# Attention of a two-layer trunk in one-engine steps, score banks used for transposes too, and a later start of branch B

## The chip, the cores and the metric

The kernel runs on one NeuronCore of a Trainium2 chip. The metric is the device time of one execution in microseconds (us), lower is better. One execution was also taken by the hardware profiler; every row below is from that one.

## What is computed

Two layers of a decoder trunk on 256 tokens of width 1024, all in float32: a SwiGLU half step, a mixer of three token branches, another SwiGLU half step, each followed by a layer norm. The mixer, cut to what matters here:

```
parts = split(x @ w_in)                      # one projection, columns shared out to A, B, C and gates
A: 3 groups of 12 heads, (window, stride) = (128,1), (512,4), (2048,16); the groups' outputs
   are combined by their softmax denominators
B: 16 query heads on 2 key heads, window 128, one learned sink per head
C: retention in chunks, then y_c = silu(parts_cg) * normed(r)
merged = g_a*(y_a @ w_proj_a) + g_b*(y_b @ w_proj_b) + g_c*(y_c @ w_proj_c);  out = merged @ w_out
```

A and B are softmax attention: scores q.k, a mask with a maximum per row, exp with a sum per row, scaling, then weights times values. A weight matrix of probabilities is transposed on TensorE (PE) before it meets the values.

## The kernel before

**The weight stream.** All the large products are cut into units: four 128-row blocks of a weight matrix, 512 columns wide (1 MB). For each unit the SP queue loads it (`dma_until`), ScalarE (ACT) rounds it to `wh` (`hi_until`, L279, "hi" below), VectorE (DVE) makes the rest `wl = ws - wh` (`lo_until`, L289, "lo" below), and PE runs three products per block. `mm_unit` (L293 to L325) is one half unit: a unit for one half of its output (t = 0 or 1), 24 matmuls of 256 columns or 12 of 512. hi and lo run three units ahead: hi stands at the end of a unit's first half, lo at the end of the second. In the mixer of one layer there are 72 units, in this order: C's values, queries and keys, B's queries, B's keys and values (`bkv`), C's swish gate (`cg`, two chunks of two units), then A's queries and keys (`aqk`, nine chunks; each ends in two rotary steps on DVE, L523 to L543, "rope" below) with A's values (`av0`, `avf`) between, then B's output projection, B's merge gates, C's gates and projection, A's gates and projection, and the last projection.

**The attention tasks.** Attention is written as Python generators. After the matmuls of a half unit, `tick` (L203) moves each running generator on to its next `yield`, and so writes its instructions on all engines right there. Each engine runs its instructions in the order in which they were written, and waits on the others by semaphores. `b_pair` (L777) is two heads of B, eight pairs per layer; `a_quad` (L695) four heads of A, three quads per layer. A pair starts at least four half units after the last start, a quad when no pair or quad runs. In a pair, the scores (PE), the masks (DVE, L639) and the exps (ACT, L643) are all written in one half unit; two half units on the scaling (ACT, L802), two further on four transposes and their copy, one on two more and their copy. A quad does the same in larger steps: near scores of two head pairs (L648), far scores (L665), the combining factors (L713 to L725), 16 scalings (L732, L736), transposes in three half units, then the values (L751).

**Banks.** Of the eight PSUM banks four (`acc`) hold the running products, one (`T`) takes transposes, two (`S`) take scores, one (`U`) takes weights times values. In `a_quad` the second transposes of a step already go to an `S` bank; in `b_pair` all go to `T`.

**The start of B.** `done_bkv` (L578) queues the eight pairs, so the first runs during the units of the swish gate `cg`. C's transposed output is queued at the first unit of gate (2, 0), L305.

Of the kernel before, what the change touches and what calls it, by code (L numbers as in the profile page):

```python
# [75 lines left out]
def mixer_chunks():  # L76
# [8 lines left out]
    aqk = lambda s, g: out.append(("aqk", (s, g), np.concatenate([roped(a_cols(3 * g, s)), roped(a_cols(3 * g + 1, s))])))  # L85
    out.append(("bkv", 0, np.concatenate([roped(OFF_KB + np.arange(128)), OFF_KB + 128 + np.arange(128), a_cols(2, 0)])))
    for n in range(2):
        out.append(("cg", n, OFF_CG + 512 * n + np.arange(512)))
    for s in range(3):
# [72 lines left out]
class Kernel:  # L162
# [4 lines left out]
    def __init__(self, ctx, tc, a):  # L167
# [12 lines left out]
        self.last = -3  # L180
# [22 lines left out]
    def tick(self, half):  # L203
# [89 lines left out]
    def mm_unit(self, u, t, mid=None, tick=False):  # L293
# [7 lines left out]
        if k0 == 0 and t == 0:  # L301
# [3 lines left out]
            elif ch["kind"] == "gate" and ch["arg"] == (2, 0):  # L305
# [272 lines left out]
    def done_bkv(self, ch, t, ps):  # L578
        nc = self.nc
        if t == 1:  # L580
            self.y[0] = self.new_y("p (b t) -> p b t", 8)
            nc.scalar.activation(self.y[0][:, 6:8], ps.rearrange("p (t c) -> p t c", t=2), AF.Copy)
            for n in range(2):
                for b in range(4):
                    self.queue(self.b_pair(n, b), "pair")
# [33 lines left out]

    def transpose_p(self, P, lo, hi, spare=False):  # L620
# [3 lines left out]
        for i in range(lo, hi):  # L624
            nc.tensor.transpose(ps[:, 128 * (i - lo):128 * (i - lo) + 128], P[:, 128 * i:128 * i + 128], self.ident)  # L625
        nc.scalar.activation(P[:, 128 * lo:128 * hi], ps[:, :128 * (hi - lo)], AF.Copy)
# [21 lines left out]
    def near_scores(self, s, b, stat):  # L648

        nc = self.nc  # L650
        k = self.aqk[s, 0]
        Sp = self.pair_scores(k[:, b], k[:, 2 + b])
# [5 lines left out]
        nc.vector.tensor_scalar(stat[:, 0, :, 2 * b:2 * b + 2], mx, -0.125, None, op0=OP.mult)  # L658
# [4 lines left out]
        return P  # L663

    def far_scores(self, s, stat):  # L665

        nc = self.nc
        Sp = self.two_S()
        for b in range(2):
            for rp in range(2):  # L670
                for g in range(2):
                    k = self.aqk[s, g + 1]
                    c0 = 256 * b + 128 * rp + 64 * g
                    for e in range(2):
                        for c in range(2):
                            r = slice(64 * e, 64 * e + 64)
                            tq = slice(64 * (2 * rp + c), 64 * (2 * rp + c) + 64)
                            nc.tensor.matmul(Sp[e][64 * c:64 * c + 64, c0:c0 + 64], k[r, b, tq], k[r, 2 + b, tq],
                                             start=True, stop=True)
        P = self.far_probs()  # L680
        mx = self.sml.tile([128, 2, 4], F32, name="fx")
        for b in range(2):
            for e in range(2):
                h = 2 * b + e
                for rp in range(2):
                    c0 = 256 * b + 128 * rp
                    self.masked(P[:, 256 * h + 128 * rp:256 * h + 128 * rp + 128], Sp[e][:, c0:c0 + 128],
                                self.mask[:, 256:384], mx[:, rp, h:h + 1])
        nc.vector.tensor_scalar(stat[:, 0], mx, -0.125, None, op0=OP.mult)
        for h in range(4):  # L690
            for rp in range(2):
                self.exp(P[:, 256 * h + 128 * rp:256 * h + 128 * rp + 128], stat[:, 0, rp, h:h + 1], stat[:, 1, rp, h:h + 1])
        return P

    def a_quad(self, s):  # L695
        nc = self.nc
# [4 lines left out]
                  for r in range(4) for t in range(2)]  # L701
        P = []
        for b in range(2):
            P.append(self.near_scores(s, b, near))
            yield
            yield
        for rows, t, to, rp in places:
            nc.gpsimd.tensor_copy(moved[to, :, rp], near[rows, :, t])
        F = self.far_scores(s, far)
        yield  # L710
        yield
        top = self.sml.tile([128, 2, 4], F32, name="top", bufs=2)
        nc.vector.tensor_tensor(top, moved[:, 0], far[:, 0], op=OP.min)  # L713
        for g, x in enumerate((moved, far)):
            nc.vector.tensor_tensor(f[:, g], top, x[:, 0], op=OP.subtract)
        nc.scalar.activation(f, f, AF.Exp)
        for g, x in enumerate((moved, far)):
# [15 lines left out]
        for h in range(4):  # L733
            for rp in range(2):
                sl = F[:, 256 * h + 128 * rp:256 * h + 128 * rp + 128]
                nc.scalar.activation(sl, sl, AF.Copy, scale=f[:, 1, rp, h:h + 1])  # L736
        yield
        yield
        for x, n in ((P[0], 6), (P[1], 6), (F, 8)):
            x = x.rearrange("p e k -> p (e k)") if n == 6 else x  # L740
            self.transpose_p(x, 0, 4)
            self.transpose_p(x, 4, n, spare=True)
            yield
        yield
        self.a_values(s, P, F)

    def a_values(self, s, P, F):
# [4 lines left out]
        for b in range(2):  # L752
# [12 lines left out]
        nc.scalar.activation(self.y[0][:, 2 * s:2 * s + 2].rearrange("p b (a r) -> p b r a", r=4),  # L765
                             U.rearrange("p b (r a) -> p b r a", r=4), AF.Copy)
# [10 lines left out]
    def b_pair(self, n, b):  # L777

        nc, l = self.nc, self.layer
        Sp = self.pair_scores(self.bq[n][:, b], self.kb[:, n])  # L780
        P = self.b_p[n, b] = self.probs((4 * n + b) % 3 == 2)
# [7 lines left out]
        nc.vector.tensor_scalar(nm, mx, -1.0, None, op0=OP.mult)  # L789
        for e in range(2):  # L790
# [5 lines left out]
        yield  # L796
# [305 lines left out]
```

## Time and profile before

| | us |
|---|---|
| median of 3 runs | 1771.24 |
| lowest and highest | 1770.83, 1771.26 |
| the profiled execution, its own time | 1771.4 |
| its span, first to last instruction | 1769.3 |
| PE busy | 1702.9 (96%) |
| DVE busy | 1064.7 (60%) |
| ACT busy | 840.0 (47%) |

The two mixers lie in the stretches 285 to 605 and 1165 to 1485 us of the span; the rest is the SwiGLU steps. A timeline row reads: start, length, engine, line, operation, tile written <- tiles read, shape, count, and in brackets how long the engine had been idle before it and what ended that. A row of a window table gives for each engine its busy time and instruction count, then PEclk (the share of TensorE's full clock of 2.4 GHz that was granted, 0.50 being 1.2 GHz).

### The profile page before, as it was taken

To read this page: it belongs to the slowest core of one execution; us is meant where nothing else is said; L and a number is where in the kernel's file an instruction comes from. 1 tells how busy PE (TensorE), PEld (TensorE's weight loads), DVE (VectorE), ACT (ScalarE), POOL (GpSimd) and SP (SyncE) were. 2 spreads that over 40 slices of the span, in tenths; PEclk is the share of its full clock that TensorE was granted. 3 is DMA by queue.
4 is the path that set the end of the run, shared out by engine and by line. 5 is a ranking of instruction groups with operands and counts; after the bars stand their busy time and mean duration, and the time that the engine had idled before them with its cause. 6 is when DMAs were issued, how large, how long until landed. Compare 5 with 4: busy or idle time off the path is not lost.

```text
span 1769.3 us, 29021 instructions
## 1 busy us (share of the span) xinstructions
PE 1702.9 (96%) x12325; PEld 1546.8 (87%) x12325; DVE 1064.7 (60%) x1536; ACT 840.0 (47%) x1207; POOL 93.1 (5%) x176
## 2 busy tenths in 40 slices
PE   9999999999889999999999999999998899999997
PEld 7998898878779998999899988978788789979985
DVE  5555677667564558554565546867666545675544
ACT  5444434654665544444344434355645675444431
POOL 0000001010211000000000000010101200000000
PEclk9999999899999999999999999999999999999998
DMA  7555543343434455555455465343433434555451
GB/s 287 214 187 193 209 162 123 139 155 121 163 118 149 171 184 193 196 210 201 167 190 211 173 222 193 143 143 121 154 141 137 165 112 180 203 184 214 175 209 47
DMA packets 49138, 303.38 MB, mean 171 GB/s; under 512 B 7025, under 2 KB 7281, under 8 KB 15089
## 3 DMA queue, kind: packets, MB, share of 16 engines
q1 hardware_dynamic: 44640, 294.12, 45.5%
q0 software_dynamic: 4224, 7.35, 1.2%
q8 instruction: 96, 1.57, 0.3%
q14 instruction: 34, 0.27, 0.0%
q10 hardware_dynamic: 144, 0.07, 0.0%
HBM read 297.31 MB, written 1.05 MB: 169 GB/s over the span
## 4 chain that ended last, share of the span: by engine, by line
PE 66%; DVE 17%; ACT 13%; issue 3%; DMA 0%; POOL 0%; SPq 0%; POOLq 0%; ACTq 0%
PE acc L320 63%; DVE wl L289 6%; ACT wh L279 5%; DVE an L639 1%; DVE slab L543 1%; ACT an L643 1%; DVE rt L523 1%; DVE rt L525 1%; DVE rt L524 1%; ACT an L802 1%; ACT af L643 1%; ACT an L732 1%; PE U L751 1%; ACT af L736 1%; DVE af L639 1%
## 5 line engine op out<-in xcount | busy, mean ns | idle before, releaser
L320 PE MATMUL acc<-xT,wh 128*128 128x256 f32 x4800 | 851.1, 280 | 0.0
L289 DVE TENSOR_TENSOR wl<-ws,wh 128x2048 fp32r<-128x2048 f32 (+1 forms) x277 | 615.5, 2240 | 269.5 <-ACT wh L279 267.7
L320 PEld LDWEIGHTS acc<-xT,wh 128*128 128x128 f32 x4800 | 736.9, 189 | 0.2
L320 PE MATMUL acc<-xT,wl 128*128 128x256 f32 x2400 | 680.1, 283 | 1.3 <-DVE wl L289 1.3
L279 ACT ACTIVATE wh<-ws 128x2048 fp32r<-128x2048 f32 (+1 forms) x277 | 518.4, 1873 | 247.1 <-PE acc L320 205.2
L320 PEld LDWEIGHTS acc<-xT,wl 128*128 128x128 f32 x2400 | 454.8, 189 | 8.9 <-issue 5.6
L320 PE MATMUL acc<-wh,xT 128*128 128x512 f32 (+1 forms) x832 | 266.5, 395 | 0.2
L320 PE MATMUL acc<-wh,hT 128*128 128x512 f32 x704 | 222.7, 396 | 0.0
L320 PEld LDWEIGHTS acc<-wh,xT 128*128 128x128 f32 x832 | 157.2, 191 | 39.9 <-issue 4.3
L320 PE MATMUL acc<-wl,xT 128*128 128x512 f32 (+1 forms) x416 | 163.1, 392 | 0.2 <-DVE wl L448 0.2
L320 PEld LDWEIGHTS acc<-wh,hT 128*128 128x128 f32 x704 | 132.4, 188 | 31.5
L320 PE MATMUL acc<-wl,hT 128*128 128x512 f32 x352 | 139.2, 395 | 0.0
L320 PE MATMUL acc<-slab,wh 128*128 128x256 f32 x704 | 127.6, 285 | 0.9 <-DVE slab L448 0.6
L490 DVE TENSOR_TENSOR h<-sa,acc 128x512 f32<-128x512 f32 x36 | 24.7, 686 | 154.2 <-PE acc L320 154.2
L320 PEld LDWEIGHTS acc<-slab,wh 128*128 128x128 f32 x704 | 110.3, 194 | 2.0 <-DVE slab L448 2.0
L320 PE MATMUL acc<-slab,wl 128*128 128x256 f32 x352 | 101.3, 288 | 7.2 <-ACT slab L447 7.2
L487 ACT ACTIVATE sa<-acc 128x512 f32<-128x512 f32 x36 | 21.5, 597 | 158.5 <-PE acc L320 158.5
L320 PEld LDWEIGHTS acc<-wl,xT 128*128 128x128 f32 x416 | 79.6, 191 | 16.7 <-DVE wl L448 0.5
L320 PEld LDWEIGHTS acc<-wl,hT 128*128 128x128 f32 x352 | 66.2, 188 | 15.6
L320 PEld LDWEIGHTS acc<-slab,wl 128*128 128x128 f32 x352 | 67.9, 193 | 9.9 <-ACT slab L447 8.6
L574 POOL DMA_DIRECT2D va<-slab x96 | 51.3, 538 | 240.7 <-ACT slab L570 238.4
L625 PE MATMUL T<-ident,an 128*128 128x128 f32 x120 | 25.6, 317 | 31.1 <-ACT an L732 12.2
(177 smaller groups left out, 1244.7 us busy)
## 6 DMA issues: line engine op xcount, KB each, us to landing
ws<-in_w_dram SPq DMA_DIRECT2D x265, 1024.0 KB, 4.8
ws<-in_w_dram SPq DMA_DIRECT2D x12, 512.0 KB, 4.2
ws<-in_w_dram SPq DMA_DIRECT2D x12, 256.0 KB, 5.7
va<-slab POOLq DMA_DIRECT2D x96, 32.0 KB, 3.0
gain<-in_ln_g_dram SPq DMA_DIRECT2D x4, 512.0 KB, 5.7
gain<-in_ln_b_dram SPq DMA_DIRECT2D x4, 512.0 KB, 7.2
slab<-in_decay_dram POOLq DMA_DIRECT2D x4, 512.0 KB, 4.6
x<-in_x_dram SPq DMA_DIRECT2D x4, 256.0 KB, 6.1
```

The lines of the kernel that those rows point to most:

```text
L279: self.nc.scalar.activation(wh[:, :n], self.staged[v][:, :n], AF.Copy)
L289: self.nc.vector.tensor_tensor(wl[:, :n], ws[:, :n], wh[:, :n].bitcast(F32), op=OP.subtract)
L320: nc.tensor.matmul(ps[:, c0:c1], a, b, start=first, stop=last, skip_group_check=len(parts) > 1)
L487: nc.scalar.activation(self.sa, ps, AF.Silu)
L490: nc.vector.tensor_tensor(h, self.sa, ps, op=OP.mult)
L523: nc.vector.stream_shuffle(t2, ps, SWAP)
L524: nc.vector.tensor_tensor(t1, ps, trig(self.cos), op=OP.mult)
L525: nc.vector.tensor_tensor(t2, t2, trig(self.sin), op=OP.mult)
L574: nc.gpsimd.dma_start(self.vf[s][p0:p0 + 32, r], self.stage[r::4, t, g])
L625: nc.tensor.transpose(ps[:, 128 * (i - lo):128 * (i - lo) + 128], P[:, 128 * i:128 * i + 128], self.ident)
L639: self.nc.vector.tensor_tensor_reduce(out=P, in0=Sp, in1=mask, op0=OP.add, op1=OP.max, scale=1.0, scalar=-3e38, accum_out=mx)
L643: self.nc.scalar.activation(P, P, AF.Exp, bias=nm, scale=0.125, accum_out=den)
```

## The change

Five things change, all in the mixer.

1. `b_pair` and `a_quad` are cut into steps of one engine each: scores in one half unit, masks in the next, exps in the next, and so on. A quad takes 15 half units from its scores to its values.
2. Starts are spaced by a table, `room`: after a pair the next pair may start three half units later and a quad seven; after a quad the next quad 15.
3. Transposes of `b_pair` go to both a lent `S` bank and `T` in the same half unit, and are copied out in the next half unit, the `S` bank first. `a_quad` packs its transposes in the same way.
4. The eight pairs are queued at the last swish gate (`done_cg`, n = 1, t = 1) instead of at `bkv`.
5. C's transposed output is queued at gate (1, 0) instead of gate (2, 0).

```
-        if kind and {"two": half == 1, "pair": self.now >= self.last + 4, "quad": not self.pairs}[kind]:
+        if kind and (half == 1 if kind == "two" else self.now >= self.room[kind]):
 ...
-            self.last = self.now
+            if kind != "two":
+                self.room = {"pair": self.now + 3, "quad": self.now + (7 if kind == "pair" else 15)}
...
-            elif ch["kind"] == "gate" and ch["arg"] == (2, 0):
+            elif ch["kind"] == "gate" and ch["arg"] == (1, 0):
                 self.queue_yT(2, 8)
...
+    def transposes(self, groups, spare):
+        ps = self.p1.tile([128, 512], F32, name="S", bufs=2) if spare else self.pt.tile([128, 512], F32, name="T")
+        copies, c = [], 0
+        for P, lo, hi in groups:
+            n = 128 * (hi - lo)
+            for i in range(lo, hi):
+                nc.tensor.transpose(ps[:, c + 128 * (i - lo):c + 128 * (i - lo) + 128], P[:, 128 * i:128 * i + 128], self.ident)
+            copies.append((P[:, 128 * lo:128 * hi], ps[:, c:c + n]))
+            c += n
+        return lambda: [nc.scalar.activation(d, x, AF.Copy) for d, x in copies]
...  a_quad:
         for b in range(2):
-            P.append(self.near_scores(s, b, near))
+            Sp = self.pair_scores(k[:, b], k[:, 2 + b])
             yield
+            P.append(self.near_max(Sp, b, near))
             yield
-        for rows, t, to, rp in places:
-            nc.gpsimd.tensor_copy(moved[to, :, rp], near[rows, :, t])
-        F = self.far_scores(s, far)
-        yield
+            self.near_exp(P[b], b, near)
+        move(0)
+        Sp = self.far_scores(s)
+        yield
+        F = self.far_max(Sp, far)
+        move(1)
         yield
...
+        for h, rp, sl in self.FAR:
+            self.exp(F[:, sl], far[:, 0, rp, h:h + 1], far[:, 1, rp, h:h + 1])
+        yield
         nc.scalar.activation(f, f, AF.Exp)
+        yield
...
+        yield
+        a = self.transposes([(x[0], 0, 4)], False), self.transposes([(x[0], 4, 6), (x[1], 0, 2)], True)
+        yield
+        for c in a:
+            c()
+        a = self.transposes([(x[1], 2, 6)], True)
+        yield
+        a()
+        a = self.transposes([(F, 0, 4)], False), self.transposes([(F, 4, 8)], True)
+        yield
+        for c in a:
+            c()
+        yield
+        U = self.a_values(s, P, F)
+        yield
...  b_pair:
         Sp = self.pair_scores(self.bq[n][:, b], self.kb[:, n])
+        yield
         P = self.b_p[n, b] = self.probs((4 * n + b) % 3 == 2)
...
         nc.vector.tensor_scalar(nm, mx, -1.0, None, op0=OP.mult)
+        yield
...
-        self.transpose_p(x, 0, 4)
-        yield
-        self.transpose_p(x, 4, 6)
+        a = self.transposes([(x, 4, 6)], True), self.transposes([(x, 0, 4)], False)
+        yield
+        for c in a:
+            c()
...  done_cg:
+        if n == 1 and t == 1:
+            for i in range(2):
+                for b in range(4):
+                    self.queue(self.b_pair(i, b), "pair")
```

What this moves, at three places. All rows are the order in which an engine's instructions stand; `an` and `af` are probabilities, `bnm` the negated row maximum of a pair, `near` and `far` the row statistics of a quad, `rt` a merge gate, `wh` the rounded weights. Line numbers shift between the two (hi L279 and L280, lo L289 and L290, exp L643 and L646, copies of transposes L626 and L629).

ACT during branch B, before: from one hi to the next, with the four-transpose copy of one pair and the exps of the next.

```order
L279 ACTIVATE wh<-ws 128x2048
L626 ACTIVATE an<-T 128x512
L643 ACTIVATE an,bden<-an,bnm 128x128
L643 ACTIVATE an,bden<-an,bnm 128x256
L794 ACTIVATE bes<-bmx,sink 128x2
```

The same place in the changed kernel, the exps of one pair and the copies of the pair ahead of it:

```order
L646 ACTIVATE an,bden<-an,bnm 128x128
L646 ACTIVATE an,bden<-an,bnm 128x256
L815 ACTIVATE bes<-bmx,sink 128x2
L629 ACTIVATE an<-S 128x256
L629 ACTIVATE an<-T 128x512
L280 ACTIVATE wh<-ws 128x2048
```

The exps now stand ahead of the copies, both copies stand together, and the one out of the `S` bank is new.

DVE in the middle of a quad, before: from the lo of one unit to the end of the combining factors (`moved` is `near` brought to the far rows' partitions by GpSimd, `aw` and `top` are factors).

```order
L289 TENSOR_TENSOR wl<-ws,wh 128x2048
L713 TENSOR_TENSOR top<-moved,far 128x8
L715 TENSOR_TENSOR af<-top,moved 128x8
L715 TENSOR_TENSOR af<-top,far 128x8
L718 TENSOR_TENSOR aw<-af,moved 128x8
L718 TENSOR_TENSOR aw<-af,far 128x8
L719 TENSOR_TENSOR top<-aw 128x8
L720 RECIPROCAL top<-top 128x8
L722 TENSOR_TENSOR af<-af,top 128x8 x2
```

The same in the changed kernel:

```order
L290 TENSOR_TENSOR wl<-ws,wh 128x2048
L722 TENSOR_TENSOR top<-moved,far 128x8
L724 TENSOR_TENSOR af<-top,moved 128x8
L724 TENSOR_TENSOR af<-top,far 128x8
L290 TENSOR_TENSOR wl<-ws,wh 128x2048
L731 TENSOR_TENSOR aw<-af,moved 128x8
L731 TENSOR_TENSOR aw<-af,far 128x8
L732 TENSOR_TENSOR top<-aw 128x8
L733 RECIPROCAL top<-top 128x8
L735 TENSOR_TENSOR af<-af,top 128x8 x2
```

A lo stands now between the two parts, so that ACT's exp of `af`, which lies between them, has a half unit of its own.

ACT in the third quad, where B's merge gates (sigmoid) run as well, before: from the exp of the factors to the second gate.

```order
L716 ACTIVATE af<-af 128x16
L725 ACTIVATE fn<-af 32x4 x8
L934 ACT_TABLE_LOAD
L934 ACTIVATE rt<-acc,gbias 128x256 x2
L279 ACTIVATE wh<-ws 128x2048
L934 ACTIVATE rt<-acc,gbias 128x256 x2
```

In the changed kernel, from the far exps of that quad to the fourth gate:

```order
L646 ACTIVATE af,far<-af,far 128x128 x8
L960 ACT_TABLE_LOAD
L960 ACTIVATE rt<-acc,gbias 128x256 x2
L280 ACTIVATE wh<-ws 128x2048
L728 ACT_TABLE_LOAD
L728 ACTIVATE af<-af 128x16
L960 ACT_TABLE_LOAD
L960 ACTIVATE rt<-acc,gbias 128x256 x2
```

Exps and sigmoids alternate here, with a table load at each turn: five loads per layer at the gates instead of one. At the swish gates four fewer stand, so that the program has 16 loads before and 16 after.

## Rows read from the trace of the kernel before

**Rows 1.** Window table of three stages: first mixer, SwiGLU steps between, second mixer.

```profile
285.00:605.00 320.00, 295.50 (x2327) 263.31 (x2326) 197.41 (x436) 191.16 (x411) 37.31 (x75) 0.96 0.39 138
605.00:1165.00 560.00, 559.71 (x3865) 515.28 (x3864) 337.09 (x334) 228.85 (x189) 12.01 (x12) 1.00 0.52 190
1165.00:1485.00 320.00, 294.35 (x2347) 262.45 (x2347) 194.61 (x425) 190.72 (x409) 34.34 (x74) 0.96 0.40 143
```

**Rows 2.** Waits of PE, first mixer: releaser, us in total, times, longest.

```profile
PE T L625 <- ACT an L732: 6.1, 2, 3.6
PE T L625 <- ACT an L802: 5.8, 4, 2.5
PE T L625 <- ACT an L626: 3.8, 3, 1.6
PE acc L320 <- ACT slab L447: 3.6, 2, 3.4
```

**Rows 3.** Timeline of PE: two waits in the first mixer, and what follows one.

```profile
326.07 1.30 PE L625 MATMUL T<-ident,an 128*128 128x128 f32 x4 [2.48 <-ACT an L802]
...
581.91 0.66 PE L625 MATMUL T<-ident,an 128*128 128x128 f32 x4 [1.55 <-ACT an L626]
...
582.55 0.36 PE L320 MATMUL acc<-xT,wl 128*128 128x256 f32 x1
```

**Rows 4.** PE in windows of 1 us: busy time (count), PEclk, DMA share, GB/s.

```profile
326.00:327.00 1.00, 0.93 (x4) 0.50 0.98 139
...
333.00:334.00 1.00, 1.00 (x11) 1.00 0.91 369
...
582.00:583.00 1.00, 1.00 (x10) 1.00 0.00 0
```

**Rows 5.** Timeline of DVE in the third quad: the lo of two units.

```profile
546.99 2.29 DVE L289 TENSOR_TENSOR wl<-ws,wh 128x2048 fp32r<-128x2048 f32 x1 [3.82 <-ACT wh L279]
...
554.87 2.29 DVE L289 TENSOR_TENSOR wl<-ws,wh 128x2048 fp32r<-128x2048 f32 x1 [4.28 <-ACT wh L279]
```

**Rows 6.** Timeline of ACT between them: near exps, a copy, the hi.

```profile
550.69 0.40 ACT L643 ACTIVATE an<-an,near 128x128 f32<-128x128 f32 x1 [3.73 <-DVE near L658]
...
552.46 0.58 ACT L945 ACTIVATE y<-acc 128x512 f32<-128x512 f32 x1
552.94 1.90 ACT L279 ACTIVATE wh<-ws 128x2048 fp32r<-128x2048 f32 x1
```

**Rows 7.** Timeline of DVE in branch B: masks, two ropes, lo, sums.

```profile
331.14 0.28 DVE L639 CUSTOM_DVE_ANT_0 af<-S,mask 128x128 f32<-128x128 f32 x1
...
332.97 0.74 DVE L523 STREAM_SHUFFLE rt<-acc 128x512 f32<-128x512 f32 x1
...
338.56 2.29 DVE L289 TENSOR_TENSOR wl<-ws,wh 128x2048 fp32r<-128x2048 f32 x1
340.76 0.16 DVE L797 TENSOR_TENSOR bden<-bden,bes 128x4 f32<-128x4 f32 x1
```

**Rows 8.** Timeline of ACT in branch B: a pair's exps, then the hi.

```profile
333.09 0.40 ACT L643 ACTIVATE af<-af,bnm 128x128 f32<-128x128 f32 x1 [2.41 <-DVE bnm L789]
...
335.24 1.90 ACT L279 ACTIVATE wh<-ws 128x2048 fp32r<-128x2048 f32 x1
```

**Rows 9.** Timeline of PE at full clock: values, scores, two half units, scores.

```profile
426.97 1.52 PE L819 MATMUL U<-an,vb 128*64 128x256 f32 x16
428.42 0.93 PE L634 MATMUL S<-slab 64*128 64x128 f32 x8
429.28 0.50 PE L320 MATMUL acc<-wh,xT 128*128 128x512 f32 x1
...
435.08 0.93 PE L634 MATMUL S<-slab 64*128 64x128 f32 x8
```

**Rows 10.** Timeline of ACT at the first merge gate: table load, sigmoids.

```profile
569.83 1.28 ACT L934 ACT_TABLE_LOAD   x1
571.12 0.84 ACT L934 ACTIVATE rt<-acc,gbias 128x256 f32<-128x256 f32 x2
```

More of the change, by code (lines that the diff above doesn't have):

```diff
@@ L88, in mixer_chunks @@
         out.append(("cg", n, OFF_CG + 512 * n + np.arange(512)))
+    aqk = lambda s, g: out.append(("aqk", (s, g), np.concatenate([roped(a_cols(3 * g, s)), roped(a_cols(3 * g + 1, s))])))
     for s in range(3):
@@ L179, in __init__ @@
         self.pairs = []
-        self.last = -3
+        self.room = {"pair": 0, "quad": 0}
         self.waiting = deque()
@@ L582, in done_bkv @@
             nc.scalar.activation(self.y[0][:, 6:8], ps.rearrange("p (t c) -> p t c", t=2), AF.Copy)
-            for n in range(2):
-                for b in range(4):
-                    self.queue(self.b_pair(n, b), "pair")
             return
@@ L677, in far_scores, with far_max @@
                             tq = slice(64 * (2 * rp + c), 64 * (2 * rp + c) + 64)
-                            nc.tensor.matmul(Sp[e][64 * c:64 * c + 64, c0:c0 + 64], k[r, b, tq], k[r, 2 + b, tq],
-                                             start=True, stop=True)
-        P = self.far_probs()
-        mx = self.sml.tile([128, 2, 4], F32, name="fx")
[L682 to L693, printed above, removed]
+                            self.nc.tensor.matmul(Sp[e][64 * c:64 * c + 64, c0:c0 + 64], k[r, b, tq], k[r, 2 + b, tq],
+                                                  start=True, stop=True)
+        return Sp
+    FAR = [(h, rp, slice(256 * h + 128 * rp, 256 * h + 128 * rp + 128)) for h in range(4) for rp in range(2)]
+    def far_max(self, Sp, stat):
+        F = self.far_probs()
+        mx = self.sml.tile([128, 2, 4], F32, name="fx")
+        for h, rp, sl in self.FAR:
+            c0 = 256 * (h // 2) + 128 * rp
+            self.masked(F[:, sl], Sp[h % 2][:, c0:c0 + 128], self.mask[:, 256:384], mx[:, rp, h:h + 1])
+        self.nc.vector.tensor_scalar(stat[:, 0], mx, -0.125, None, op0=OP.mult)
+        return F
     def a_quad(self, s):
@@ L701, in a_quad, with move @@
                   for r in range(4) for t in range(2)]
+        k = self.aqk[s, 0]
+        def move(i):
+            for rows, t, to, rp in places:
+                nc.gpsimd.tensor_copy(moved[to, i, rp], near[rows, i, t])
         P = []
         for b in range(2):
-            P.append(self.near_scores(s, b, near))
+            Sp = self.pair_scores(k[:, b], k[:, 2 + b])
             yield
+            P.append(self.near_max(Sp, b, near))
             yield
-        for rows, t, to, rp in places:
-            nc.gpsimd.tensor_copy(moved[to, :, rp], near[rows, :, t])
-        F = self.far_scores(s, far)
+            self.near_exp(P[b], b, near)
+        move(0)
+        Sp = self.far_scores(s)
         yield
+        F = self.far_max(Sp, far)
+        move(1)
         yield
@@ L715, in a_quad @@
             nc.vector.tensor_tensor(f[:, g], top, x[:, 0], op=OP.subtract)
+        for h, rp, sl in self.FAR:
+            self.exp(F[:, sl], far[:, 0, rp, h:h + 1], far[:, 1, rp, h:h + 1])
+        yield
         nc.scalar.activation(f, f, AF.Exp)
+        yield
         for g, x in enumerate((moved, far)):
@@ L732, in a_quad @@
                     nc.scalar.activation(sl, sl, AF.Copy, scale=fn[:, t, 2 * b + e:2 * b + e + 1])
[L733 to L736, printed above, removed]
         yield
+        for h, rp, sl in self.FAR:
+            nc.scalar.activation(F[:, sl], F[:, sl], AF.Copy, scale=f[:, 1, rp, h:h + 1])
         yield
-        for x, n in ((P[0], 6), (P[1], 6), (F, 8)):
-            x = x.rearrange("p e k -> p (e k)") if n == 6 else x
-            self.transpose_p(x, 0, 4)
-            self.transpose_p(x, 4, n, spare=True)
-            yield
-        yield
-        self.a_values(s, P, F)
+        x = [p.rearrange("p e k -> p (e k)") for p in P]
+        a = self.transposes([(x[0], 0, 4)], False), self.transposes([(x[0], 4, 6), (x[1], 0, 2)], True)
+        yield
+        for c in a:
[10 more added lines that the diff above has]
+        yield
+        nc.scalar.activation(self.y[0][:, 2 * s:2 * s + 2].rearrange("p b (a r) -> p b r a", r=4),
+                             U.rearrange("p b (r a) -> p b r a", r=4), AF.Copy)
     def a_values(self, s, P, F):
```

26 lines of the change are left out of this document (7 added, 19 removed).

## The prediction

> **What bounds the kernel now.** I read the window table by stage first, because shares over the whole span hide where PE stands. Between the mixers PE is busy for 559.71 of 560 us at the full clock; each mixer leaves it idle for 24.5 and 25.65 us of 320, together 50.2, at a mean granted clock of 0.96 [rows 1]. So the SwiGLU steps have nothing to give, and a change to the mixer can only work on what PE loses there. The second loss is in the clock. The window table by 1 us shows 0.50 right after a wait of 2.48 us and 1.00 again at 333, that is 1.2 GHz for some 7 us; 4 matmuls start in the us at 326, and 10 and 11 in one at the full clock; after a wait of 1.55 us the clock was 1.00 [rows 3, 4]. A mean of 0.96 over 320 us is 12.8 us per mixer, 25.6 in both (22.4 to 28.8 with the rounding of that figure). Idle time and clock together: 75.8 us.
>
> Then I read what PE waits for. In the first mixer 15.7 of the 24.5 us are transposes to bank T that wait for ACT, behind a scaling or behind a copy of transposes, and 3.6 are B's projection, which waits for ACT's splits of B's output [rows 2]. The second mixer has the same code and nearly the same idle time. All these instructions are short. They are late because ACT and DVE wait for each other in a ring: the lo of one unit starts at 546.99, the masks stand behind it, the exps wait 3.73 us for them and start at 550.69, the hi follows at 552.94, and the next lo, which waited 4.28 us for that hi, starts at 554.87 [rows 5, 6]. One turn is 7.88 us per unit. PE needs for a unit two half units of 2.90 us (5.80 us lie between 429.28 and 435.08) and one set of scores of 0.86, that is 6.7 [rows 9]. The attention falls behind by 1.2 us per unit, until PE gets to something that depends on it.
>
> **The change, part by part.** Operations are neither added nor dropped, but for the grouping of copies and of the GpSimd moves; PE's work stays what it is. The time of the profiled execution is 1771.4 (span 1769.3 and 2.1 around it), 0.2 above the median, and the sum is made against it. With no loss in the mixers it would be 1771.4 - 50.2 - 25.6 = 1695.6. That is the floor, and a reason why nothing here gains more: outside, PE is full. I then add what I expect to stay.
>
> *One engine per half unit.* Masks are written a half unit ahead of the exps, ahead of the lo of that half, so the hi behind the exps no longer waits for masks that stand behind the lo before. The ring of 7.88 us now has two units of PE time (13.4 us) to turn in. That removes the waits on scalings. B's splits no longer stand behind 16 scalings in one half unit either, as these are now in half units of their own; the 3.6 us at the projection go with that. I take both as gone, and keep their price in the bounds.
>
> *Pairs every three half units instead of four.* DVE has, per three half units with ropes, one set of masks at 1.83 (331.14 to 332.97), 1.5 ropes at 2.80 (two in the 5.59 to 338.56), 1.5 lo at 2.20 and about 0.4 of small operations: 9.7 us [rows 7]. PE takes 3 x 2.90 + 0.86 for scores, 0.64 for six transposes and half of 1.45 for values: 10.9 [rows 3, 9]. So DVE is 89% full. It keeps up, but a set of masks can stand behind a rope and a lo (5.0 us), and the margins are short.
>
> *A lent score bank.* The transposes of a pair go to an S bank; the next pair but one needs both S banks one half unit later. The copy that frees the bank stands on ACT behind the exps of the pair between (2.15 us, 333.09 to 335.24 [rows 8]); its 256 columns are a third of what these exps treat, so at most 0.7. Laying the rows end to end from the first pair on, I find the copy 0 to 2 us ahead of PE, shortest at the last pairs, where ropes and masks have piled up on DVE. I take 0.2 us for each of 16 pairs, 3 us; the bounds are 0 and, as for the waits on scalings of today (5.8 us in 4 [rows 2]), 1.45 each, 23 us.
>
> *Quads.* The first two per layer meet only ropes and splits. Laid out in the same way, far scores wait for the masks of the second near pair by 0.4 us; I take 0.5 each, 2 us for four quads, bounds 0 and 3.05 each (the mean of the two waits on L732 [rows 2]). GpSimd's moves now stand in part behind the issue of A's value transfers, for which I find two half units of room: nothing, as nothing but the factors on DVE waits for them.
>
> *The later start of B.* The pairs leave the swish gates, so four table loads of 1.28 us per layer leave there, beside PE work in any case. The third quad moves back by about two units, into the merge gates: four more turns between exp and sigmoid there, 4 x 1.28 = 5.1 us of ACT work [rows 10], and each gate's product on DVE waits behind one. DVE carries this on to the lo and to the quad's factors. I lay that out to 0.5 to 2 us of waiting at the third quad's transposes: 1.5 each, 3 us. At the first gate the sigmoid started 0.01 us behind the end of its table load, and the load right at the end of the work before it [rows 10]. The Trainium skill says more (ScalarE: Activation LUTs, What ACT_TABLE_LOAD costs): a load of about 1283 ns and a drain of about 1380, 2.66 us per switch, and a kernel should do all of one set before it switches, which speaks against this part. The row shows the load and no drain; with the page's price the third quad would be some 5.5 us later per layer.
>
> *C's transposed output, two chunks earlier.* Its splits wait for T, free by then, and the projection that reads them comes six units later: nothing, or a few tenths if a split misses its half unit.
>
> *Clock.* One fall in one of the two layers, 7 us at 0.50, costs 3.5 us; bounds none and four falls, 14.
>
> Sum: 1695.6 + 3 + 2 + 3 + 3.5 = 1707.
>
> **The rivals.**
>
> *The waits move to the banks.* Each pair waits once for a lent bank, at the 1.45 us of today's waits: 23 us instead of 3, and one fall of the clock more per layer, 7 us. 1695.6 + 23 + 2 + 3 + 10.5 = 1734. For it: DVE at 89%, margins of 0 to 2 us, strict order on ACT. Against it: the pile on DVE empties in each chunk without ropes (`avf`, `av0`).
>
> *The merge gates.* The five loads delay the third quad by all of their 5.1 us, and the clock falls once: 5.1 + 3.5 - 1.5 = 7.1 per layer more, 1721. For it: ACT has there in six half units five loads (6.4 us), three hi (5.7), two sets of near exps (1.77 each), four pairs of sigmoids (3.4) and the far exps (2.9, as 2.15 for 768 columns), 21.9 us [rows 6, 8, 10], and PE takes six times 2.90 and two sets of scores, 19. Against it: the quad's transposes come three half units behind the last of them. With the 2.66 us that the Trainium skill gives for a switch (same section) it would be 1732; the row speaks for 1.28.
>
> *The banks close a ring: slower.* If the two ropes and the lo (7.8 us) stand ahead of each set of masks, one turn is scores 0.86, masks 1.83, exps 2.15, copy 0.7 and those 7.8: 13.3 us against the 10.9 that PE needs. PE then waits 2.4 us at each of 16 pairs, and if each such wait brings a fall (3.5) that is 94 us, and 1695.6 + 94 + 8 = 1798. Without falls it is 1742. It decides, faster or slower, from about 4.2 us per pair. Against it: ropes come in two of every four half units, and the masks are written ahead of the rope of their half unit.
>
> *It doesn't do what it says.* Some needs stay in one half unit (values that free a buffer for masks, the lent bank). If these rule, the waits are today's: 1771.
>
> **How the numbers follow.** The forecast, 1697 to 1720, has 0.69; the banks 0.15, about 1734; the gates 0.10, about 1721; the slower ring 0.03; no change 0.02; below 1697 0.01. The range 1697 to 1731 leaves out the upper half of the banks' case and the slower ones, about 0.14. A difference of 0.2% (3.5 us) is about what a measurement of this kernel can tell from none: faster 0.95, same 0.02, slower 0.03.
>
> **What would show it.** In the changed profile PE's idle time in a mixer should be under 7 us instead of 25, with a granted clock of 0.99 or more; DVE and ACT should be equally busy in fewer us. The waits of PE on scalings (L823, L744) should be gone. What is left should read S or T waiting for ACT copies (L629) or DVE masks (L642), none much over 1 us. Waits of scores in B on copies, 1 us and more, would show the banks; waits of the third quad's transposes with a clock of 0.50 after them the gates. It would be wrong in its base if PE's matmuls themselves went slower in the mixer at the full clock, or if lo came late and PE waited for `wl`.

## The result, and the profile after

The changed kernel takes 1692.38 us (median of 4 runs, 1690.82 to 1692.55), the kernel before took 1771.25 beside it (1770.83 to 1771.39): a ratio of 0.9553, 95% interval 0.9537 to 0.957, or 78.9 us less. The forecast was 1707 with a range from 1697 to 1731: the direction and the places were right, the time came out 4.6 us below the range (a chance of 0.01 by the prediction), and below the 1695.6 that the prediction called the floor. That last point is what the experiments had to explain. The profiled execution took 1690.82 us, with a span of 1689.0.

The page of the changed kernel, its engines' busy times and the granted clock in 40 slices. Before, PE's share was 96%, and the clock's row had an 8 in the first mixer besides the one at the end.

```profile
PE 1670.1 (99%) x12325; PEld 1526.8 (90%) x12325; DVE 1064.6 (63%) x1536; ACT 840.3 (50%) x1207; POOL 118.6 (7%) x224
PEclk9999999999999999999999999999999999999998
```

The window table of the two mixers and, last, of the stretch of branch B's pairs; the columns are those of [rows 1] (PE, PEld, DVE, ACT, POOL, granted clock, DMA).

```profile
285.00:585.00 300.00, 298.85 (x2502) 273.01 (x2502) 207.79 (x442) 200.24 (x418) 48.96 (x99) 1.00 0.44 159
...
1145.00:1445.00 300.00, 298.86 (x2600) 277.22 (x2599) 203.32 (x412) 197.90 (x418) 43.88 (x96) 1.00 0.44 161
320.00:410.00 90.00, 90.00 (x704) 81.50 (x703) 76.33 (x179) 62.45 (x146) 8.60 (x16) 1.00 0.40 147
```

PE is idle for 1.15 us in a mixer where it was idle for 24.5 and 25.65 [rows 1], and the clock, at 0.96 before, is at 1.00. During the pairs PE is busy for all of 90 us, with DVE at 76.33, 85% (the prediction had laid out 89%).

What PE still waits for between 200 and 1600 us (us in total, times, longest), against [rows 2]:

```profile
PE T L626 <- ACT an L744: 1.2, 2, 0.6
PE T L626 <- ACT an L629: 0.7, 2, 0.3
PE S L458 <- DVE x L480: 0.3, 2, 0.2
```

The first two are once per layer each, at one place, the third quad at the merge gates, in the timeline of PE:

```profile
552.14 1.02 PE L626 MATMUL T<-ident,an 128*128 128x128 f32 x4 [0.60 <-ACT an L744]
...
560.68 0.66 PE L626 MATMUL T<-ident,af 128*128 128x128 f32 x4 [0.33 <-ACT an L629]
```

### The profile page after: what moved, and what is told of

It reads as the page before. It is cut to its first block, busy times and chain, and to the rows that moved or that the text cites. A ratio compares the mean times of both kernels' runs of the same rounds, so it can differ in the third digit from the quotient of the medians.

```text
span 1689.0 us, 29101 instructions
## 1 busy us (share of the span) xinstructions
PE 1670.1 (99%) x12325; PEld 1526.8 (90%) x12325; DVE 1064.6 (63%) x1536; ACT 840.3 (50%) x1207; POOL 118.6 (7%) x224
## 5 line engine op out<-in xcount | busy, mean ns | idle before, releaser
L290 DVE TENSOR_TENSOR wl<-ws,wh 128x2048 fp32r<-128x2048 f32 (+1 forms) x277 | 615.5, 2240 | 165.5 <-ACT wh L280 165.0
L280 ACT ACTIVATE wh<-ws 128x2048 fp32r<-128x2048 f32 (+1 forms) x277 | 519.0, 1875 | 247.8 <-PE acc L321 208.0
L321 PE MATMUL acc<-slab,wh 128*128 128x256 f32 x704 | 123.7, 278 | 0.0
L321 PEld LDWEIGHTS acc<-wl,xT 128*128 128x128 f32 x416 | 78.2, 188 | 16.2 <-DVE wl L449 0.5
L475 POOL TENSOR_TENSOR rs<-rs,nhalf 128x1 f32<-128x1 f32 x12 | 11.7, 971 | 806.0 <-DVE rs L474 806.0
```

The costliest lines, as they stand in the source:

```text
L280: self.nc.scalar.activation(wh[:, :n], self.staged[v][:, :n], AF.Copy)
L290: self.nc.vector.tensor_tensor(wl[:, :n], ws[:, :n], wh[:, :n].bitcast(F32), op=OP.subtract)
L321: nc.tensor.matmul(ps[:, c0:c1], a, b, start=first, stop=last, skip_group_check=len(parts) > 1)
L475: nc.gpsimd.tensor_tensor(rs, rs, self.nhalf[:, 0:1], op=OP.pow)
```

## The experiments

Each run was timed beside the kernel before (1771.6 to 1772.0 there, 1771.25 beside the changed kernel), and the four executions of one kernel lie 0.5 to 5.8 us apart, so a difference of 2 us or less between medians says nothing by itself. Most runs undo one part of the changed kernel or several together; the later ones put a part by itself into the old surroundings, and the last goes on from the change. Line numbers are each kernel's own. "From start to start" is the distance between the starts of two neighbouring matmuls, less what the same pair of forms takes in the changed kernel (its median there).

**What a wait costs: the lent bank taken away.** Both groups of a pair's transposes go to bank T:

```
-        a = self.transposes([(x, 4, 6)], True), self.transposes([(x, 0, 4)], False)
+        self.transposes([(x, 4, 6)], False)()
+        c = self.transposes([(x, 0, 4)], False)
```

> The changed kernel with the lent bank taken away: both groups of a pair's transposes go to bank T, the second behind the copy of the first in the same half unit, so PE gets there what ACT makes in the same half unit, 16 times in all. Theory A (every such place is a wait): 16 waits of about 0.8 us, as the kernel before shows at 357, 419 and 457 (0.82 to 0.87 us from start to start), 13 us, without a fall of the clock: 1705. If what a wait costs is more than the idle time that stands beside it, as the missing 8 us of the forecast suggest, the time grows by about 0.2 us per wait more than PE's idle time does, 3 us of the 13. Rival (ACT is half idle there and the copy is ready): under 0.2 us each, 1692 to 1695.

Measured: 1704.13 us, 11.8 more than the changed kernel. The timeline of PE at the first pair, in this run and then, for the same place, in the changed kernel:

```profile
332.66 0.38 PE L626 MATMUL T<-ident,an 128*128 128x128 f32 x2
333.57 0.66 PE L626 MATMUL T<-ident,an 128*128 128x128 f32 x4 [0.54 <-ACT an L629]
```

```profile
332.44 0.38 PE L626 MATMUL S<-ident,an 128*128 128x128 f32 x2
332.66 0.60 PE L626 MATMUL T<-ident,an 128*128 128x128 f32 x4
```

The bracket says 0.54 us. From start to start it is 333.57 - 332.66 = 0.91 against 332.66 - 332.44 = 0.22: 0.69. In all 16 places the bracket is 0.53 or 0.54 and the distance 0.70. The clock stayed at 1.00 there. 16 x 0.70 is 11.2 us, 16 x 0.53 is 8.5, and the time grew by 11.8 (11.3 when each is taken against the kernel before beside it): it is nearer to the starts, though the spread of the runs alone would not rule out 8.5. What decides is that the starts are recorded, while the end of a matmul is modelled in the profile: the bracket counts from that end, and 332.66 + 0.38 = 333.04 lies later than 332.88, where the next matmul would have started without the wait. Theory A holds, and with it the part on the price.

**The pairs' ring, put back.** Scores, masks and exps of a pair stand in one half unit again (the `yield` behind the scores goes ahead of them, the one between masks and exps goes behind both).

> The changed kernel with the pairs' scores, masks and exps back in one half unit (all else of its order and its spacing of three half units stays). Theory A (the ring of lo, masks, exps and hi between DVE and ACT): one turn per pair is masks 1.83, exps 2.15, hi 1.9, lo 2.2 and 1.5 ropes, 4.2, in all 12.3 us against 10.9 of PE, so the attention falls 1.4 us behind with each pair, some 11 us in eight; with 2 to 3 us of room PE waits 8 us per layer, with falls of the clock 12: about 1710 to 1717. Rival (a pair meets a mask only once in three half units, so the ring never closes and what held the kernel before were scalings and copies): 1692 to 1696, and PE idle in a mixer under 3 us.

Measured: 1690.64 us (ratio 0.9542, 0.9528 to 0.9557), not to be told from the changed kernel, with the same four waits and PE again busy for 90.00 of the 90 us of the pairs. Theory A falls for the pairs: their masks and exps apart gain nothing by themselves.

**The pairs' denominators, put back.** The `yield` between the reciprocal and the four scalings goes ahead of the sum.

> The changed kernel with one part of the pairs undone: the sum and reciprocal of the denominators (DVE) and the four scalings (ACT) stand in one half unit again, one half unit ahead of the transposes, as they are now. Theory A (in the kernel before the scalings waited 4.45 us at 308.13 for a reciprocal that stood behind a lo of 2.28 us, and PE then 1.92 us for the scalings): in every second pair a lo stands ahead of the reciprocal, so 8 of 16 pairs make PE wait 1 to 2 us, 8 to 16 us and some falls of the clock, 1700 to 1715. Rival (as with masks and exps of the pairs, which gave nothing when they were put back together, ACT has room between): 1691 to 1695.

Measured: 1693.27 us (0.9553, 0.9537 to 0.9569), the same four waits. Theory A falls here too.

**All three at once.** The edits of the last three runs together.

> The changed kernel with three parts of the pairs undone at once, each of which was undone alone before: masks and exps in one half unit with the scores (1690.6 alone), reciprocal and scalings in one (1693.3 alone), both groups of transposes in bank T with a copy between (1704.1 alone). The late start and the spacing of three half units stay. Theory A (the parts add up, the bank is all that the pairs' steps gain): about 1704, waits of 0.70 us from start to start at 16 places, 1702 to 1707. Rival (either separation alone gives ACT the room, so the waits on scalings return only when both are gone, as with the old pairs, where 8 waits on scalings and 6 on copies are left): 1715 to 1730, PE waiting for scalings.

Measured: 1749.38 us, 57.0 more than the changed kernel, where the parts alone add up to 11. Neither expectation holds: the sum is far off, and PE waits for copies, not for scalings. It waits at the same 16 places as without the lent bank, but for up to 4.0 us, and the clock falls in eight stretches (16.2 us lost from start to start). The wait for bank T, in the timelines of DVE, ACT and PE:

```profile
390.45 0.29 DVE L642 CUSTOM_DVE_ANT_0 af<-S,mask 128x128 f32<-128x128 f32 x1 [4.24 <-PE S L637]
...
392.47 0.41 ACT L646 ACTIVATE af<-af,bnm 128x128 f32<-128x128 f32 x1 [4.67 <-DVE bnm L809]
...
394.61 1.90 ACT L280 ACTIVATE wh<-ws 128x2048 fp32r<-128x2048 f32 x1
396.41 0.58 ACT L843 ACTIVATE y<-U 128x512 f32<-128x512 f32 x1
396.88 0.37 ACT L629 ACTIVATE an<-T 128x256 f32<-128x256 f32 x1
...
397.30 1.12 PE L626 MATMUL T<-ident,an 128*128 128x128 f32 x4 [3.66 <-ACT an L629]
```

The two transposes whose copy this is were started at 393.26. Their copy stands on ACT behind the next pair's exps, which start at 392.47 only, as the masks start at 390.45, behind scores that were issued with them; then come the hi and a copy of values. In the run without the lent bank alone, the next pair's exps are written a half unit later than here, so the copy stands ahead of them and found ACT idle. Timeline of ACT at the first pair of that run:

```profile
333.13 0.38 ACT L629 ACTIVATE an<-T 128x256 f32<-128x256 f32 x1 [3.11 <-PE T L626]
333.42 0.39 ACT L646 ACTIVATE an<-an,bnm 128x128 f32<-128x128 f32 x1
```

There the short copy costs 0.70. With a second bank PE doesn't need the copy yet. So the bank alone takes the wait away, the later exps alone leave 0.70 of it, and with both gone it is up to 4.0: the parts don't add up. What the third edit, the denominators, adds to this was not run apart.

**The early start, put back alone, and with the three.** B's pairs are queued at the key and value chunk again instead of the last swish gate.

> The changed kernel with one part undone: branch B's pairs are queued again at B's key and value chunk, eight half units earlier, ahead of the swish gates. Theory A (the prediction's: the later start costs and gives PE nothing, the staggered half units do it all): within 2 us of the changed kernel's 1692.4, perhaps 1 to 2 us less, as the third quad leaves the merge gates, where the changed trace shows its only waits (0.76 and 0.49 us from start to start, in each layer). Theory B (the start matters, because the pairs' exps meet the swish gates on ACT): the two waits that the kernel before shows there come back, 2.09 us at 306 and 2.64 us at 323, with the clock's falls behind them (1.7 and 3.4 us lost), about 10 us per layer, 1712.

Measured: 1696.22 us, 3.8 more: neither theory's number. Its four executions took 1694.34 to 1697.07 us at mean granted clocks from 0.997 down to 0.995, so a part of the 3.8 is falls of the clock that not every execution had. There is one wait at the swish gates per layer, not the two old ones, and one at the third quad. Timelines of ACT and PE, and two windows (PE's busy time comes first, the clock last but two):

```profile
313.76 1.28 ACT L872 ACT_TABLE_LOAD   x1
315.06 0.60 ACT L872 ACTIVATE rt<-acc 128x512 f32<-128x512 f32 x1
315.55 0.38 ACT L632 ACTIVATE an<-S 128x256 f32<-128x256 f32 x1
...
315.98 0.92 PE L640 MATMUL S<-kb,slab 64*128 64x128 f32 x6 [1.56 <-ACT an L632]
...
540.52 0.66 PE L629 MATMUL T<-ident,an 128*128 128x128 f32 x4 [1.50 <-DVE slab L449]
```

```profile
316.00:317.00 1.00, 1.00 (x7) 0.67 (x8) 1.00 (x2) 1.00 (x2) 0.00 (x0) 1.00 0.00 0
...
318.00:319.00 1.00, 1.00 (x6) 1.00 (x6) 0.96 (x6) 0.26 (x2) 0.00 (x0) 0.50 0.00 0
```

This is the wait for a lent bank that the prediction feared, near its price of 1.45, though once per layer and not at each pair: the copy that frees S stands behind exps and the table load of a swish gate. The later start takes the pairs out of the swish gates. The wait at 540.52 is the third quad's for bank T, behind the lo of C's output; the hi that this lo needs stands on ACT behind eight scalings of that quad.

> As the run with three parts of the pairs undone, and the early start at the key and value chunk too (alone 1696.2), so that only the spacing, the new quads and C's earlier output are left of the change. Theory A (parts add up): 1704 + 4 = 1708, 1704 to 1712. Rival (the early start is what makes the old grouping dear, since scalings and reciprocals then share the half units with the swish gates and C's statistics): 1720 or more, with waits on scalings of about 2 us near 310 and 326 in the first layer, as the kernel before and the run with the old pairs have them.

Measured: 1757.38 us, 8.0 more than the three alone, twice what the start costs by itself; the longest wait is 7.1 us (at 320.0). Theory A's sum fell with the run before. The rival's number fits, but there is only one wait on scalings per layer (1.8 us at 312); the rest is bank T again. Nor is this the kernel before in branch B: with the old pairs, start and spacing the kernel takes 1730.05 us (below), 27 less. The old pairs spread their transposes over two half units and start every four; here both groups go through bank T in one half unit, every three. So the 57.0 us are the price of three edits at this spacing, not what the new pairs gain.

**The quads' ring, put back.** Scores, masks and exps of the two near pairs and of the far ones stand in one half unit each.

> The changed kernel with the quads' scores, masks and exps back in one half unit, three times per quad (two near, one far), all else as it is. Theory A (the ring, 7.88 us per unit against 6.7 of PE): three turns make a quad 3.5 us late, and PE waits for it at the quad's first transposes, about 3 us as in the kernel before (mean of two 3.05), in six quads: 18 us and up to six falls of 1.7 to 3.4 us, 1710 to 1728. Rival (the scalings now have half units of their own, so there is room for 3.5 us): 1692 to 1698.

Measured: 1721.74 us, 29.4 more, as theory A has it in sum. It isn't spread over six quads, though. The first waits of PE:

```profile
PE T L626 <- ACT an L744: 12.1, 2, 6.1
PE acc L321 <- ACT slab L448: 6.5, 4, 2.2
PE T L945 <- DVE slab L449: 2.6, 2, 1.3
```

Only the third quad of a layer waits for its scalings, in the first layer here, with two rows of ACT ahead of it:

```profile
548.54 1.28 ACT L646 ACT_TABLE_LOAD   x1 [3.09 <-DVE far L691]
...
556.99 1.28 ACT L728 ACT_TABLE_LOAD   x1
...
566.66 1.30 PE L626 MATMUL T<-ident,an 128*128 128x128 f32 x4 [6.05 <-ACT an L744]
```

The first two quads cost PE nothing themselves, but B's projection waits for splits of B's output that stand on ACT behind their exps, as in [rows 2]. Four stretches of 6.8 us at 0.50 cost some 10 us more, from start to start. The ring isn't alone here: with the exps elsewhere in the order, a layer has seven table loads at the merge gates, where the changed kernel has five, 2.6 us more of ACT work ahead of the third quad's scalings. The run doesn't part the two.

**The quads' factors, put back.** Exp, small steps, copies of factors and near scalings in one half unit, the far scalings as they are.

> The changed kernel with one part of the quads undone: the exp of the factors, DVE's small steps on them, the 8 copies of the factors and the near scalings stand in one half unit again, two exchanges between ACT and DVE in one half unit instead of none; the masks and exps stay apart. Theory A (each product got in the half unit in which it is made is a wait for PE): ACT waits for DVE's six small steps, which stand behind a lo (2.2 us) or a rope (2.8), so the scalings end 1 to 3 us later and PE waits that long at each quad's first transposes, six times: 6 to 18 us, 1698 to 1710, with the third quad of each layer worst, where there is no room today. Rival (only the third quad is short of room): 2 waits of 1 to 3 us, 1694 to 1699.

Measured: 1693.88 us, 1.5 more, which is within the spread of the runs, and just below the rival's range. The trace has two waits of 1.4 us per layer, in the second and the third quad, of the far transposes for the copy that frees bank T, and none for the scalings, so neither theory's mechanism is there.

**The pairs alone, and the quads alone.** First the kernel before with `b_pair` and `transposes` of the changed one:

> The kernel before with branch B's new steps alone: staggered half units and the lent bank, but B's old start, the old spacing of four half units and the old quads. If the losses add up by place: the waits of the kernel before up to 440 us in the first mixer, 10.5 us from start to start, and three falls of the clock there, 6.8 us, are the pairs', 17.3 per layer, so 1771.5 less 34.6 is 1737, or some 4 more for the early start (the run with the start undone). Rival (the quads' lateness begins in the pairs, so that with the pairs in time the quads wait less too): 1725 or less. Rival (the pairs gain nothing without the later start and the closer spacing): over 1755.

Measured: 1748.15 us, 23.5 less than before and outside all three forecasts. The window table, first of this run, then of the kernel before for its pairs:

```profile
285.00:450.00 165.00, 164.70 (x1217) 144.12 (x1216) 121.01 (x285) 101.89 (x221) 25.93 (x43) 1.00 0.43 154
450.00:605.00 155.00, 135.23 (x1193) 125.78 (x1192) 82.29 (x157) 93.82 (x193) 12.26 (x32) 0.91 0.37 133
```

```profile
285.00:440.00 155.00, 145.69 (x977) 125.01 (x976) 106.38 (x244) 85.68 (x174) 15.86 (x19) 0.96 0.37 133
```

During the pairs PE is full, so the expected gain of 17 us per layer is there; behind them it is lost again in part. The largest wait, in the timelines of ACT and PE:

```profile
564.42 2.43 ACT L749 ACTIVATE af<-af 128x128 f32<-128x128 f32 x8
566.87 1.28 ACT L950 ACT_TABLE_LOAD   x1
568.17 0.84 ACT L950 ACTIVATE rt<-acc,gbias 128x256 f32<-128x256 f32 x2
568.90 1.91 ACT L279 ACTIVATE wh<-ws 128x2048 fp32r<-128x2048 f32 x1
570.70 0.84 ACT L950 ACTIVATE rt<-acc,gbias 128x256 f32<-128x256 f32 x2
571.41 0.61 ACT L626 ACTIVATE an<-T 128x512 f32<-128x512 f32 x1
...
572.08 1.12 PE L935 MATMUL T<-ident,y 128*128 128x128 f32 x4 [8.40 <-ACT an L626]
```

A copy of 0.61 us, on which bank T hangs, stands on ACT behind eight scalings, a table load, sigmoids and a hi. The reverse, the changed kernel with B's old pairs, start and spacing:

> The reverse: the changed kernel with branch B's steps, start and spacing of four half units as in the kernel before, so that the new quads (and C's output two chunks earlier) stand alone. By place: the quads' stretch of the kernel before, from 440 us on, lost 16.2 us of waits and 6.8 of clock per layer, 23, so 1771.5 less 46 is 1725. Added to the pairs alone it should give the whole gain of 79 within a few us. Rival (parts overlap: each alone removes only waits that the other's would still bring): both gains together well under 79, this one at 1740 or more.

Measured: 1730.05 us, 41.6 less than before, between the two forecasts. Its window table:

```profile
285.00:440.00 155.00, 143.79 (x973) 122.89 (x973) 109.71 (x247) 87.95 (x174) 15.86 (x19) 0.98 0.39 138
440.00:605.00 165.00, 163.85 (x1539) 153.81 (x1538) 99.20 (x199) 117.78 (x250) 35.27 (x80) 1.00 0.45 160
```

Behind the old pairs, from 440 on, PE is nearly full. Both gains are 65.1 us; the 14 missing from the whole gain are about what the pairs alone gave back behind the pairs (about 60 us lost there from start to start in both layers, against 46 in the kernel before). The quads together with C's earlier output carry the larger part. The closer spacing of the pairs was not undone by itself.

**C's transposed output, earlier.** The run of the pairs alone, with `queue_yT(2, 8)` at gate `(1, 0)`:

> The kernel before with branch B's new steps (as in the run of the pairs alone, 1748.15) and C's transposed output two chunks earlier. In the run without it the longest wait of all, 8.4 us in each layer, is that of C's first transposes for bank T, at the gate of branch C, behind the copy of the third quad's transposes, which stands on ACT behind 8 scalings, a table load, four sigmoids and a hi. Theory A (the earlier place matters, because it takes C's four turns of bank T out of the way of the late third quad; the prediction costed it at nothing): the waits at C's transposes go, 9.8 us from start to start per layer, and the fall of the clock of 13.7 us behind them, up to 6.8 us lost: 1715 to 1728. Rival (it is the quad that is late, and the projection or the quad's own next transposes wait for the same copy): 1745 to 1750.

Measured: 1738.40 us, 9.8 less. The waits of PE at C's transposes, first without this edit, then with it:

```profile
PE T L935 <- ACT an L626: 17.7, 4, 8.4
PE T L935 <- ACT af L626: 0.6, 2, 0.3
```

```profile
PE T L935 <- DVE slab L448: 11.4, 4, 3.2
```

Theory A is right in direction, with less than half of the 20 to 33 us that it gave. The waits behind the quad's copies go, others for DVE's splits of C's output come, and the quads' own transposes wait as long as before (10.7 us without the edit, 11.7 with it). In the changed kernel itself this part was not undone, so its share there stays open.

**Going on: the third quad later.**

```
+        if s == 2:
+            yield
+            yield
         x = [p.rearrange("p e k -> p (e k)") for p in P]
```

> The changed kernel, with the third quad's transposes, copies and values two half units later (nothing waits for its output until the gates of branch A). Theory A (the only waits left in a mixer are the third quad's first transposes behind the near scalings and its far transposes behind a copy, 0.76 and 0.49 us from start to start, because the merge gates' sigmoids, table loads and products delay ACT and DVE): both go, 2.5 us in two layers, 1689.9, and PE idle in a mixer about 0.6 us. Rival (the wait moves on, to the splits of A's output or to the slabs): no difference, 1692.4.

Measured: 1686.79 us (1686.25 to 1688.42), a ratio of 0.9522, 0.9508 to 0.9536, against 0.9537 to 0.957 of the changed kernel: the fastest of all. No wait is left in the mixers, in the window table:

```profile
285.00:585.00 300.00, 300.00 (x2521) 275.26 (x2519) 209.94 (x451) 201.73 (x420) 51.24 (x99) 1.00 0.44 161
1145.00:1445.00 300.00, 300.00 (x2615) 279.61 (x2614) 204.21 (x415) 199.41 (x419) 43.98 (x96) 1.00 0.45 164
```

It gained 5.6 us, where theory A had 2.5. The four waits are 2.5 of it from start to start; another 2 us lie in distances between starts that are each too short to show a bracket, and where the rest lies was not settled.

## Why the prediction was right, and where it failed

*The floor: failed, and the largest error.* The step was 1771.4 - 50.2 - 25.6 = 1695.6. With all waits gone the kernel takes 1686.8, 8.8 less. The clock's term nearly holds: the stretches at 0.50 in both mixers lose 25.6 us by the clock's record and 27.5 by the starts of the matmuls in them, and none is left. The idle term was mis-sized. In the timeline of PE of the kernel before, 31 gaps over 0.25 us add up to 48.7 us by their brackets and to 55.0 from start to start, 0.2 us more for each, as the run without the lent bank shows by itself (0.53 against 0.70, and the time follows the 0.70). That is 6.3 of the 8.8, and the clock's 1.9 are another part; the rest, under 1 us, is within the spread of the runs. So here the idle time of PE by the profile is less than what the waits cost, and "a reason why nothing here gains more" was wrong in its base.

*The remains: 11.5 added, 5.6 needed.* Pairs' lent banks, 3: measured 0; no scores wait for a copy. First quads, 2: measured 0. Falls of the clock, 3.5: 0 in the mixers. Third quad at the merge gates, 3: 1.9 us of idle time in four waits, 2.5 from start to start, at the place and of the kind that the prediction named. Together with the floor, 8.8 too high, the remains, 5.9 too high, make up the 14.6 us of the miss. The two errors had the same sign, so they couldn't cancel.

*The ring: right for the quads, wrong for the pairs.* The turn of 7.88 us was read in the third quad [rows 5, 6] and taken for that of all the attention. Put back in the quads it costs 29.4 us, with two table loads more per layer; put back in the pairs alone, nothing. A pair meets masks once in three half units; that DVE and ACT catch up between is argued from this, not shown. That the waits on scalings go is right (two of 0.6 us are left); that keeping exps and masks apart does it is shown for the quads alone, and there for the third.

*Parts undone one by one don't add up.* The pairs' three edits cost 0, 0 and 11.8 us when undone alone, and 57.0 together. The prediction gave the gain to masks and exps in half units of their own and took the lent bank for a risk alone. Of the three the bank is the one whose undoing costs time by itself, and how much depends on where the exps stand.

*The later start and C's earlier output: their gain was put at nothing.* The start was priced by its cost alone, 3 us at the third quad; undone it makes the kernel 3.8 us slower, and 8.0 slower with the three edits. C's earlier place gave 9.8 us in one other setting; in the changed kernel no wait at C's transposes is left, as the prediction had it, and what the place gains there is open. The rows at 313.76 and at 566.87 above show what both avoid: a copy that PE waits for, behind a table load and gates.

*The table load.* In the run of the pairs alone a load took 1.28 us, began 0.02 us after the scalings ahead of it ended (564.42 + 2.43) and was followed 0.02 us later by a sigmoid, as in [rows 10]. The Trainium skill gives 2.66 us per switch, with a drain (ScalarE: Activation LUTs, What ACT_TABLE_LOAD costs); the rows here show half of that, and the sum with 1.28 was the right one. Its advice, to do all of one set before switching, stands on the same page under Rules for kernel authors, not in the section that the prediction names. The only waits left in the mixers stood where the sets alternate, at the merge gates, which agrees with it; that the loads make them was not tested.

*The rivals.* The waits didn't move to the banks; with the early start put back one per layer did, 1.56 us against the 1.45 forecast. The merge gates took 2.5 us and no fall of the clock, not 14. The slower ring of the banks didn't close: PE is busy for all of the pairs' 90 us, and DVE had 15% to spare, not 11.

## What to carry to other kernels

Read a wait of PE from the start of one matmul to the start of the next, against the same pair where nothing waits, and expect it to be longer than the bracketed idle time; a floor made by subtracting idle time came out too high here. When engines pass work in a circle, count how many links of it stand in one step of the order: one alone may be free, while three together cost five times the sum of their single prices here, so undo parts in groups before you call one useless. And look for short copies that free a bank and stand on a queue behind long work: the place where PE waits is theirs, whatever the long work is.

## What the runs showed of the hardware that was not expected

The length of a wait alone did not decide whether the clock fell. A wait of 1.56 us at 315.98 was followed by 0.50, 1.2 GHz, in the window from 318 on (above), though the prediction's 1.55 had left it at 1.00 [rows 3, 4]. And in the run of the quads alone a wait of 2.27 us was followed by no fall; the rows are PE's timeline, then the window table:

```profile
369.43 0.76 PE L849 MATMUL U<-an,vb 128*64 128x256 f32 x5 [2.27 <-ACT an L640]
```

```profile
370.00:372.00 2.00, 2.00 (x11) 1.51 (x10) 2.00 (x3) 0.60 (x1) 0.00 (x0) 1.00 0.00 0
372.00:374.00 2.00, 2.00 (x10) 1.64 (x9) 1.50 (x3) 0.37 (x2) 0.00 (x0) 1.00 0.00 0
374.00:376.00 2.00, 2.00 (x10) 1.54 (x10) 0.00 (x0) 2.00 (x5) 0.00 (x0) 1.00 0.80 242
```

Nor did each execution of one kernel have the same falls: the four of the run with the early start had mean granted clocks of 0.995, 0.995, 0.996 and 0.997, at 1697.07, 1697.02, 1695.41 and 1694.34 us. So a fall could not have been told from the wait's length, and the prediction's one fall was a guess that didn't come.
